# One level of Strassen's recursion in a gate-and-up projection, with the weight differences on GpSimd

## The chip, the cores and the metric

The kernel runs on one core of a Trainium2 chip. That core has a matrix engine (TensorE, PE in the profile), VectorE (DVE), ScalarE (ACT), GpSimd (POOL) and SyncE (SP), which here only issues transfers. They share an on-chip memory, SBUF, of 128 partitions; matmul results go to PSUM, eight banks of 128 x 512 f32. Each engine works its own queue of instructions in order, and waits on semaphores for the others. The metric is the device time of one execution in microseconds.

## What is computed

A hybrid layer (a recurrent branch and an attention branch, merged, then a gated feed-forward), and behind it a second attention layer, on 256 tokens of width 2048, all in f32. The part that matters here is the feed-forward of the first layer:

```python
def _layer(h, ...):
    ...
    h = h + merged @ w_o
    gate, up = jnp.split(_rms(h, n2) @ w_gu, 2, axis=-1)
    return h + (jax.nn.silu(gate) * up) @ w_dn
```

`w_gu` is 2048 x 11264, gate and up each 5632 columns; `w_dn` is 5632 x 2048.

## The kernel before

**Three matmuls for one.** f32 operands are split into two parts of type fp32r, `hi` (a rounded copy, made on ScalarE) and `lo` (what is left, a subtraction on VectorE); that is `split`, lines 219 to 221. `mm3` (line 270) then adds hi x hi, hi x lo and lo x hi into one PSUM bank. All products run in this way, so most matmuls of the profile carry line 263, that of the helper `mm`.

**Weights.** `wload` (line 225) loads one chunk, 256 rows by 512 columns or 512 KB, into a raw tile [128, 1024] by a transfer on SyncE's queue, and splits it. From the output projection on there are two rings of three raw tiles, `raw` and `raw2`, drawn alternately, and three pairs of `hi` and `lo`. The loads and splits are issued with a priority offset `AHEAD` of 300, so that the program's scheduler puts them ahead of the matmuls before them.

**A projection.** `gemm_b` (line 286) takes two banks of tag `g`, one for each half of 128 tokens (t = 0, 1). For each chunk it calls `mm3` for two row blocks and both halves: 12 matmuls of 128x512 on one split chunk. Banks: four of tag `g`, two of `q`, two of `f`.

**The feed-forward** (lines 1009 to 1045). The normalised activations, transposed, are `fgh` and `fgl`, [128, 16, 256] each: 16 row blocks by 256 tokens. The loop at line 1018 makes two passes, over 6 and then 5 groups of 512 hidden columns. A group calls `gemm_b` for the gate (8 chunks, line 1025), makes tanh on ScalarE and the silu on VectorE out of PSUM (lines 1028, 1029), calls it for the up part (line 1030) and multiplies from PSUM (line 1032). `nat_to_t` (line 928) transposes the 512 columns on TensorE into two banks taken from `q` and `f` in turn and splits them again. After each pass the down projection adds its part to the residual `hn` (`add_rows`, line 984).

The order of the instructions on each engine is made when the program is built, by a list scheduler with a model of time.

Of the kernel before, what the change touches and what calls it, by code (L numbers as in the profile page):

```python
# [196 lines left out]
def body(tc, a, out):  # L197
# [5 lines left out]
    with ExitStack() as top:  # L203
# [94 lines left out]
            return [p[:, :n] for p in ps]  # L298

        ch = lambda w, g, c0, c1: [w[g, c] for c in range(c0, c1)]  # L300


        vec = T(cp, [128, NVEC], "vec")
# [621 lines left out]
            flip[0] ^= 1  # L925
            return bank("qf"[flip[0]])

        def nat_to_t(src, hi, lo, kt0, gain=None):

            n = src.shape[2] // 128  # L930
            for k in range(0, n, 2):
                m = min(2, n - k)
                ps = bank2()
                for j in range(m):
                    for t in range(2):
                        o = 256 * j + 128 * t
                        tr(ps[:, o:o + 128], src[:, t, 128 * (k + j):128 * (k + j) + 128], ident)
                if gain is None:
                    split(ps[:, :256 * m].rearrange("p (a b) -> p a b", b=256), hi[:, kt0 + k:kt0 + k + m], lo[:, kt0 + k:kt0 + k + m])
                    continue  # L940
                for j in range(m):
                    kt = kt0 + k + j
                    pj = ps[:, 256 * j:256 * j + 256]
                    S.activation(hi[:, kt], pj, AF.Copy, scale=vc(gain, kt))
                    V.scalar_tensor_tensor(out=lo[:, kt], in0=pj, scalar=vc(gain, kt), in1=hi[:, kt].bitcast(F32), op0=ALU.mult, op1=ALU.subtract)
# [5 lines left out]
        with ExitStack() as ph:  # L951
            mp = ph.enter_context(tc.tile_pool(name="mp", bufs=2))
            mh, ml = unit("Y0", yp), unit("Y1", yp)
            br = []
            for k_, w_, n_, p_ in ((0, "w_a", "X3", yp), (1, "w_b", "X1", xp)):
                u_ = T(p_, [128, 2, 8, 256], n_, F32R)
                br.append((a[w_], u_))
            part = T(xp, [128, 2, D], "X0")
            for b in (1, 0):
                w_, u_ = br[b]  # L960
                for k in range(2):
                    raw = T(wp, [128, 1024], "raw", bufs=3)
                    nc.sync.dma_start(raw.rearrange("p (q f) -> p q f", f=512), ydr[b][2 * k:2 * k + 2].rearrange("q p f -> p q f"))
                    r3_ = raw.rearrange("p (k t) -> p k t", t=256)
                    split(r3_, u_[:, 0, 4 * k:4 * k + 4], u_[:, 1, 4 * k:4 * k + 4])
                for n in range(4):
                    g_ = T(wp, [128, 2, 512], "gate", bufs=1)
                    G.dma_start(g_, gdr[4 * b + n])
                    ps = gemm_b(ch(w_, n, 0, 4), lambda kt: (u_[:, 0, kt], u_[:, 1, kt]))
                    sl = slice(512 * n, 512 * n + 512)  # L970
                    if b == 0:
                        with tc.issue_after(latest[0].ins):
                            nc.sync.dma_start(hn[:, :, sl], a["xn"][:, :, sl])
                    for t in range(2):
                        if b:
                            V.tensor_tensor(out=part[:, t, sl], in0=g_[:, t], in1=ps[t], op=ALU.mult)
                        else:
                            V.tensor_tensor(out=g_[:, t], in0=g_[:, t], in1=ps[t], op=ALU.mult)
                            V.tensor_tensor(out=part[:, t, sl], in0=part[:, t, sl], in1=g_[:, t], op=ALU.add)
                    if b == 0:  # L980
                        nat_to_t(part[:, :, sl], mh, ml, 4 * n)
            sq2 = T(cp, [128, 2, 4], "sq2")

            def add_rows(ps, n, stat, p):
                sl = slice(512 * n, 512 * n + 512)
                for t in range(2):
                    V.tensor_tensor(out=hn[:, t, sl], in0=ps[t], in1=hn[:, t, sl], op=ALU.add)
                    if stat is not None:
                        junk = T(p, [128, 512], "junk")
                        S.activation(junk, hn[:, t, sl], AF.Square, accum_out=stat[:, t, n:n + 1])  # L990

            def rstd(stat, tag, n):
                r = T(cp, [128, 2], tag)
                V.tensor_reduce(out=r, in_=stat, axis=AX.X, op=ALU.add)
                S.activation(r, r, AF.Sqrt, bias=e6, scale=1.0 / n)
                V.reciprocal(r, r)
                return r

            gh, gl = unit("X0", xp), unit("X1", xp)
            more_raw.extend((yp, True))  # L1000
            for n in range(4):
                ps = gemm_b(ch(a["w_o"], n, 0, 8), lambda kt: (mh[:, kt], ml[:, kt]))
                add_rows(ps, n, sq2, mp)
                nat_to_t(hn[:, :, 512 * n:512 * n + 512], gh, gl, 4 * n, "n2")
            r2 = rstd(sq2, "r2", D)


        with ExitStack() as ph:
# [6 lines left out]
            units = (("X2", yp), ("X3", yp), ("Y0", yp), ("Y1", yp), ("X2", yp), ("X3", yp))  # L1015
            ui = 0
            fgh, fgl = gh, gl
            for p0, p1 in ((0, 6), (6, 11)):
                hid = []
                for n in range(p0, p1):  # L1020
                    if (n - p0) % 2 == 0:
                        hid.append(T(units[ui][1], [128, 2, 8, 256], units[ui][0], F32R))
                        ui += 1
                    xg = lambda kt: (fgh[:, kt], fgl[:, kt])
                    pgt = gemm_b(ch(a["w_gu"], n, 0, 8), xg)
                    th = T(fp, [128, 2, 512], "th")
                    for t in range(2):
                        S.activation(th[:, t], pgt[t], AF.Tanh, scale=r2h[:, t:t + 1])  # L1028
                        V.scalar_tensor_tensor(out=th[:, t], in0=th[:, t], scalar=1.0, in1=pgt[t], op0=ALU.add, op1=ALU.mult)
                    pup = gemm_b(ch(a["w_gu"], 11 + n, 0, 8), xg)  # L1030
                    for t in range(2):
                        V.scalar_tensor_tensor(out=th[:, t], in0=pup[t], scalar=r2s[:, t:t + 1], in1=th[:, t], op0=ALU.mult, op1=ALU.mult)
                    hu = hid[-1]
                    nat_to_t(th, hu[:, 0], hu[:, 1], 4 * ((n - p0) % 2))
                last = p1 == 11
                if last:
                    gh, gl = unit("X0", xp), unit("X1", xp)
                for n in range(4):
                    ps = gemm_b(ch(a["w_dn"], n, 2 * p0, 2 * p1), lambda kt: (hid[kt // 8][:, 0, kt % 8], hid[kt // 8][:, 1, kt % 8]))
                    add_rows(ps, n, sq3 if last else None, fp)  # L1040
                    if last:
                        nat_to_t(hn[:, :, 512 * n:512 * n + 512], gh, gl, 4 * n, "np")
# [267 lines left out]
```

## Time and profile before

| what | us |
|---|---|
| median of three runs (2030.91 to 2040.93) | 2037.02 |
| the profiled execution | 2035.52 |
| its span in the profile | 2033.8 |
| one gate-and-up group, from one to the next in the chain | 44.4 |

A row of the profile gives the line, the engine, the operation, the tiles written and read with their shapes, and the count; behind the first bar the busy time in us, the mean of one in ns; behind the second the idle time of that engine just before it and what ended it. In rows of the timeline the first two numbers are start and length in us; neighbours of one kind are merged, with their count. A matmul's duration there overlaps the next one's. In a row of the waits, the total, the count and the longest follow the names.

### The profile page before, as it was taken

The page shows a single profiled execution, that of the slowest core. Times are in us where ns is not written, and L with a number is a line of the kernel's source. Part 1 is how long each engine was busy: PE and PEld are TensorE (multiplying, and loading weights), DVE is VectorE, ACT ScalarE, POOL GpSimd, SP SyncE. Part 2 cuts the span into 40 slices and gives each one's busy share as a digit, 9 for nine tenths or more (in the row PEclk, how much of TensorE's full clock was granted, in tenths as well). Part 3 has the DMA queues.
Part 4 walks back from the last instruction along what each step waited for, and adds up shares of the span by engine and source line. Part 5 has one row for each costly group of instructions (what it writes and reads, how often), then busy time and mean ns, then how long its engine had stood idle before and what let it go on. Part 6 is the DMA issues. An engine that isn't in the chain of part 4 may idle for free.

```text
span 2033.8 us, 29647 instructions
## 1 busy us (share of the span) xinstructions
PE 1981.4 (97%) x11410; PEld 1698.3 (84%) x11410; DVE 1223.3 (60%) x2188; ACT 954.3 (47%) x1290; POOL 152.6 (8%) x226
## 2 busy tenths in 40 slices
PE   8998989999999999999999999999999999999998
PEld 7997879879767778888888888888888889998886
DVE  6787767778755456555555544555555655656555
ACT  6545445546444434554444433444444565444443
POOL 3131041221310000000000000000000000000000
PEclk9999999999999999999999999999999999999999
DMA  6644354444456676555555555555555565444564
GB/s 210 188 131 135 113 162 139 149 152 156 127 157 224 219 265 239 187 187 192 190 186 188 194 189 194 196 187 186 190 193 186 178 205 190 146 135 156 186 193 143
DMA packets 119566, 363.27 MB, mean 179 GB/s; under 512 B 28848, under 2 KB 29648, under 8 KB 119424
## 3 DMA queue, kind: packets, MB, share of 16 engines
q1 hardware_dynamic: 114576, 345.40, 51.7%
q0 software_dynamic: 4848, 15.97, 2.7%
q8 instruction: 89, 1.46, 0.3%
q14 instruction: 53, 0.43, 0.1%
HBM read 351.72 MB, written 9.60 MB: 178 GB/s over the span
## 4 chain that ended last, share of the span: by engine, by line
PE 86%; DVE 6%; DMA 4%; ACT 2%; issue 1%; POOL 1%; SPq 0%; DVEq 0%; ACTq 0%
PE g L263 78%; PE f L263 3%; DVE lo L221 3%; PE q L263 3%; DMA raw<-in_w_b 1%; PE f L267 1%; ACT hi L220 1%; PE q L267 1%; DVE xx L658 1%; DMA raw<-in_w_a 1%; POOL p L854 1%; DVE c L655 1%; DMA raw<-in_w_g 0%; DMA x<-in_xT 0%; DVE gt L589 0%
## 5 line engine op out<-in xcount | busy, mean ns | idle before, releaser
L221 DVE TENSOR_TENSOR lo<-raw,hi 128x1024 fp32r<-128x1024 f32 (+1 forms) x635 | 772.9, 1218 | 604.4 <-ACT hi L220 599.9
L263 PE MATMUL g<-hi,X 128*128 128x512 f32 (+1 forms) x3344 | 1045.5, 391 | 4.3 <-ACT X L220 1.7
L220 ACT CAST hi<-raw 128x1024 fp32r<-128x1024 f32 (+1 forms) x635 | 661.4, 1042 | 817.5 <-PE g L263 679.9
L263 PEld LDWEIGHTS g<-hi,X 128*128 128x128 f32 x3344 | 626.7, 188 | 135.0 <-issue 3.1
L263 PE MATMUL g<-lo,X 128*128 128x512 f32 (+1 forms) x1672 | 652.9, 391 | 2.7 <-DVE lo L221 2.7
L263 PE MATMUL g<-X,hi 128*128 128x272 f32 (+3 forms) x2176 | 430.3, 296 | 3.3 <-ACT hi L220 3.1
L263 PEld LDWEIGHTS g<-lo,X 128*128 128x128 f32 x1672 | 314.3, 188 | 67.5 <-DVE lo L221 5.1
L263 PEld LDWEIGHTS g<-X,hi 128*128 128x128 f32 (+1 forms) x2176 | 347.1, 193 | 10.7 <-ACT hi L220 3.6
L263 PE MATMUL g<-X,lo 128*128 128x272 f32 (+3 forms) x1088 | 318.2, 292 | 1.5 <-DVE lo L221 1.4
L263 PEld LDWEIGHTS g<-X,lo 128*128 128x128 f32 (+1 forms) x1088 | 209.4, 192 | 2.8 <-DVE lo L221 2.4
L263 PE MATMUL g<-hi,Y 128*128 128x512 f32 x544 | 171.0, 391 | 0.0
L263 PEld LDWEIGHTS g<-hi,Y 128*128 128x128 f32 x544 | 102.2, 188 | 20.7
L263 PE MATMUL g<-lo,Y 128*128 128x512 f32 x272 | 106.7, 392 | 0.0
L1049 POOL DMA_DIRECT2D cst<-in_cst x1 | 0.5, 541 | 832.6 <-DMA raw<-in_w_cq 832.6
L263 PEld LDWEIGHTS g<-lo,Y 128*128 128x128 f32 x272 | 51.1, 188 | 10.3
L854 POOL TENSOR_SCALAR p<-ckb,cq,qs 128x144 f32<-128x144 f32 (+1 forms) x32 | 45.6, 1434 | 66.2 <-DVE c L655 28.3
L655 DVE TENSOR_TENSOR c<-hq,xx 108x42 f32<-108x42 f32 (+31 forms) x236 | 40.3, 204 | 9.7 <-DMA hq<-hd 9.4
L658 DVE TENSOR_TENSOR xx<-xx,c 108x42 f32<-108x42 f32 (+31 forms) x236 | 40.8, 203 | 0.4
L420 POOL TENSOR_TENSOR d<-z 128x272 f32<-128x272 f32 (+3 forms) x28 | 22.4, 800 | 86.8 <-DVE z L419 56.0
L870 ACT ACTIVATE p<-p,fst,qs 128x144 f32<-128x144 f32 (+1 forms) x32 | 17.7, 553 | 7.8 <-DVE fst L869 7.6
L267 PE MATMUL f<-ident,p 128*128 128x128 f32 (+1 forms) x64 | 14.5, 333 | 6.6 <-DVE p L873 4.0
L1028 ACT ACTIVATE th<-g,r2h 128x512 f32<-128x512 f32 x22 | 15.1, 685 | 9.9 <-PE g L263 9.9
(425 smaller groups left out, 1342.9 us busy)
## 6 DMA issues: line engine op xcount, KB each, us to landing
raw<-in_w_gu SPq DMA_DIRECT2D x176, 512.0 KB
raw<-in_w_A SPq DMA_DIRECT2D x98, 512.0 KB
raw<-in_w_dn SPq DMA_DIRECT2D x88, 512.0 KB
raw<-in_w_g SPq DMA_DIRECT2D x64, 512.0 KB
raw<-in_w_o SPq DMA_DIRECT2D x32, 512.0 KB
raw<-in_w_qk SPq DMA_DIRECT2D x32, 512.0 KB
raw<-in_w_out SPq DMA_DIRECT2D x32, 512.0 KB
raw<-in_w_b SPq DMA_DIRECT2D x16, 512.0 KB
```

The costliest lines, as they stand in the source:

```text
L220: S.copy(hi, src)
L221: V.tensor_tensor(out=lo, in0=src, in1=hi.bitcast(F32), op=ALU.subtract)
L263: P.matmul(o, l, r, start=start, stop=stop, **k)
L267: P.transpose(o, i, eye)
L420: G.tensor_tensor(out=d[:m, t1:], in0=z[:m, t1:L], in1=z[:m, 1 + t1:], op=ALU.subtract)
L655: V.tensor_tensor(out=t_, in0=hs[:108, j, j + 1:].unsqueeze(1).to_broadcast([108, k_, w]), in1=xs[:, :, j:j + 1].to_broadcast([108, k_, w] ...
L658: V.tensor_tensor(out=xs[:, :, j + 1:], in0=xs[:, :, j + 1:], in1=t_, op=ALU.add)
L854: G.tensor_scalar(out=m_, in0=ckb[:, 2 * j + e, :n], scalar1=cq[:, t, hg:hg + 1], scalar2=qs[:, 0, t, 2 * j + e:2 * j + e + 1], op0=ALU.su ...
L870: S.activation(m_, m_, AF.Exp, bias=st[:, 1, sidx:sidx + 1], scale=qs[:, 1, t, h:h + 1], accum_out=st[:, 2, sidx:sidx + 1])
L1028: S.activation(th[:, t], pgt[t], AF.Tanh, scale=r2h[:, t:t + 1])
L1049: G.dma_start(cst2, a["cst2"])
```

## The change

Gate and up columns are now made together by `gemm_s`, which takes the 8 gate chunks `c1` and the 8 up chunks `c2` of a group. The 8 chunks form four pairs (c, c + 4). Pairs 1 and 3 run as before: each chunk split by `wload`, 48 matmuls a pair. Pairs 0 and 2 run by Strassen's scheme in Winograd's form: the two halves of tokens by the two chunks of rows is one 2 x 2 block matrix, the two chunks by gate and up another. Seven products stand in for eight; each product has six matmuls (two row blocks, three matmuls each).

For that, the four raw weight chunks of a pair are combined on GpSimd by four subtractions of 128x1024 f32 (`t1`, `b12` in place, `t2`, `t4`), and each of the seven right operands is split into hi and lo. The left operands need sums of the activations, made once before the first group by `sums_x` on GpSimd (four combinations a pair) and split. The products go to all eight banks; m1, m5, m6 and m7 are combined by one copy on ScalarE and four additions on VectorE after pair 2, and m2, m3, m4 and m8 are added at the end of pair 3. Gate and up then lie in SBUF tiles `e0` and `e1`, and the silu reads them there. The transposes of a group use a single bank of tag `f`; `junk`, `th`, `e0` and `e1` have one buffer each.

```diff
+        def raw_w(src):
+            more_raw[1] = not more_raw[1]
+            raw = T(wp, [128, 1024], "raw", bufs=3) if more_raw[1] else T(more_raw[0], [128, 1024], "raw2", bufs=3)
+            latest[0] = nc.sync.dma_start(raw.rearrange("p (n m) -> p n m", m=512), src)
+            return raw
+
+        def halves_w(raw):
+            hi, lo = (T(wp, [128, 1024], k, F32R, bufs=3) for k in ("hi", "lo"))
+            split(raw, hi, lo)
+            return tuple(t.rearrange("p (n m) -> p n m", m=512) for t in (hi, lo))
+
+        def sums_x(hi, lo, c, h, p, dst):
+            af = T(p, [128, 2, 2, 256], "T", bufs=3)
+            for k in range(2):
+                ks = slice(2 * (c + k * h), 2 * (c + k * h) + 2)
+                G.tensor_tensor(out=af[:, k], in0=hi[:, ks].bitcast(F32), in1=lo[:, ks].bitcast(F32), op=ALU.add)
+            blk = lambda t, k: af[:, k, :, 128 * t:128 * t + 128]
+            sf = T(p, [128, 4, 2, 128], "T", bufs=3)
+            G.tensor_tensor(out=sf[:, 0], in0=blk(1, 0), in1=blk(1, 1), op=ALU.add)
+            G.tensor_tensor(out=sf[:, 1], in0=sf[:, 0], in1=blk(0, 0), op=ALU.subtract)
+            G.tensor_tensor(out=sf[:, 2], in0=blk(0, 0), in1=blk(1, 0), op=ALU.subtract)
+            G.tensor_tensor(out=sf[:, 3], in0=blk(0, 1), in1=sf[:, 1], op=ALU.subtract)
+            split(sf, dst[0], dst[1])
+
+        def gemm_s(c1, c2, hi, lo, sx, p, e0, e1):
+            h = len(c1) // 2
+            m1, m6, m7, m5 = (bank("g") for _ in range(4))
+            m2, m3, m4, m8 = bank("q"), bank("q"), bank("f"), bank("f")
...
+            for c in range(h):
+                end = c == h - 1
+                if c in sx:
+                    with tc.high_priority(offset=AHEAD):
+                        b12, b11, b22, b21 = (raw_w(v) for v in (c2[c], c1[c], c2[c + h], c1[c + h]))
+                        t1, t2, t4 = (T(p, [128, 1024], "T", bufs=3) for _ in range(3))
+                        G.tensor_tensor(out=t1, in0=b12, in1=b11, op=ALU.subtract)
+                        G.tensor_tensor(out=b12, in0=b22, in1=b12, op=ALU.subtract)
+                        G.tensor_tensor(out=t2, in0=b22, in1=t1, op=ALU.subtract)
+                        G.tensor_tensor(out=t4, in0=b21, in1=t2, op=ALU.subtract)
+                    s_ = [[v[:, k] for v in sx[c]] for k in range(4)]
+                    stop = c == last
+                    for ps, l, r, st in (
+                        (m1, blk(0, c), b11, stop), (m2, blk(0, c + h), b21, False), (m3, s_[3], b22, False),
+                        (m5, s_[0], t1, stop), (m7, s_[2], b12, stop), (m6, s_[1], t2, stop), (m4, blk(1, c + h), t4, False),
+                    ):
+                        with tc.high_priority(offset=AHEAD):
+                            r = halves_w(r)
+                        prod(ps, l, r, st)
+                    if stop:
+                        S.copy(e0[:, 0], m1)
+                        V.tensor_tensor(out=e0[:, 1], in0=m6, in1=e0[:, 0], op=ALU.add)
+                        V.tensor_tensor(out=e1[:, 0], in0=m5, in1=e0[:, 1], op=ALU.add)
+                        V.tensor_tensor(out=e0[:, 1], in0=m7, in1=e0[:, 1], op=ALU.add)
+                        V.tensor_tensor(out=e1[:, 1], in0=m5, in1=e0[:, 1], op=ALU.add)
+                    continue
+                for src, k, ps in ((c1[c], c, (m2, m4)), (c1[c + h], c + h, (m2, m4)), (c2[c], c, (m3, m8)), (c2[c + h], c + h, (m3, m8))):
+                    r = wload(src, 2, 512)
+                    for t in range(2):
+                        prod(ps[t], blk(t, k), r, end and k >= h)
+                    if end and k >= h:
+                        e_ = e0 if ps[0] is m2 else e1
+                        for t in range(2):
+                            V.tensor_tensor(out=e_[:, t], in0=ps[t], in1=e_[:, t], op=ALU.add)
...
-                    xg = lambda kt: (fgh[:, kt], fgl[:, kt])
-                    pgt = gemm_b(ch(a["w_gu"], n, 0, 8), xg)
-                    th = T(fp, [128, 2, 512], "th")
+                    e0, e1 = T(fp, [128, 2, 512], "e0", bufs=1), T(wp, [128, 2, 512], "gate", bufs=1)
+                    gemm_s(ch(a["w_gu"], n, 0, 8), ch(a["w_gu"], 11 + n, 0, 8), fgh, fgl, sx, fp, e0, e1)
+                    th = T(fp, [128, 2, 512], "th", bufs=1)
                     for t in range(2):
-                        S.activation(th[:, t], pgt[t], AF.Tanh, scale=r2h[:, t:t + 1])
-                        V.scalar_tensor_tensor(out=th[:, t], in0=th[:, t], scalar=1.0, in1=pgt[t], op0=ALU.add, op1=ALU.mult)
-                    pup = gemm_b(ch(a["w_gu"], 11 + n, 0, 8), xg)
-                    for t in range(2):
-                        V.scalar_tensor_tensor(out=th[:, t], in0=pup[t], scalar=r2s[:, t:t + 1], in1=th[:, t], op0=ALU.mult, op1=ALU.mult)
+                        S.activation(th[:, t], e0[:, t], AF.Tanh, scale=r2h[:, t:t + 1])
+                        V.scalar_tensor_tensor(out=th[:, t], in0=th[:, t], scalar=1.0, in1=e0[:, t], op0=ALU.add, op1=ALU.mult)
+                        V.scalar_tensor_tensor(out=th[:, t], in0=e1[:, t], scalar=r2s[:, t:t + 1], in1=th[:, t], op0=ALU.mult, op1=ALU.mult)
                     hu = hid[-1]
-                    nat_to_t(th, hu[:, 0], hu[:, 1], 4 * ((n - p0) % 2))
+                    nat_to_t(th, hu[:, 0], hu[:, 1], 4 * ((n - p0) % 2), ps=bank("f"))
```

More of the change, by code (lines that the diff above doesn't have):

```diff
@@ new lines, in gemm_s, with prod @@
+        def gemm_s(c1, c2, hi, lo, sx, p, e0, e1):
+            h = len(c1) // 2
+            m1, m6, m7, m5 = (bank("g") for _ in range(4))
+            m2, m3, m4, m8 = bank("q"), bank("q"), bank("f"), bank("f")
+            used = set()
+            def prod(ps, l, r, stop=False):
+                for j in range(2):
+                    mm3(ps, [v[:, j] for v in l], [v[:, j] for v in r], id(ps) not in used, stop and j == 1)
+                    used.add(id(ps))
+            blk = lambda t, c: [v[:, 2 * c:2 * c + 2, 128 * t:128 * t + 128] for v in (hi, lo)]
+            last = max(c for c in range(h) if c in sx)
+            for c in range(h):
[32 more added lines that the diff above has]
+                            V.tensor_tensor(out=e_[:, t], in0=ps[t], in1=e_[:, t], op=ALU.add)
@@ L926, in bank2, with nat_to_t @@
             return bank("qf"[flip[0]])
-        def nat_to_t(src, hi, lo, kt0, gain=None):
-            n = src.shape[2] // 128
+        def nat_to_t(src, hi, lo, kt0, gain=None, ps=None):
+            n, one = src.shape[2] // 128, ps
             for k in range(0, n, 2):
                 m = min(2, n - k)
-                ps = bank2()
+                ps = bank2() if one is None else one
                 for j in range(m):
@@ L988, in add_rows @@
                     if stat is not None:
-                        junk = T(p, [128, 512], "junk")
+                        junk = T(p, [128, 512], "junk", bufs=1)
                         S.activation(junk, hn[:, t, sl], AF.Square, accum_out=stat[:, t, n:n + 1])
@@ L1017, in body @@
             fgh, fgl = gh, gl
+            sx = {}
+            for c in (0, 2):
+                sx[c] = tuple(T(fp, [128, 4, 2, 128], f"S{c}", F32R, bufs=2) for _ in range(2))
+                sums_x(fgh, fgl, c, 4, fp, sx[c])
             for p0, p1 in ((0, 6), (6, 11)):
```

## The prediction

> **What bounds the kernel now.** I read the page's first part, then the chain that ended last, then the busy time by stretches of one gate-and-up group each, then the waits.
>
> ```profile
> span 2033.8 us, 29647 instructions
> PE 1981.4 (97%) x11410; PEld 1698.3 (84%) x11410; DVE 1223.3 (60%) x2188; ACT 954.3 (47%) x1290; POOL 152.6 (8%) x226
> ```
> ```profile
> 931.04 43.31 PE g L263 x191
> 975.46 43.33 PE g L263 x191
> ```
> ```profile
> core 0: us, PE busy (x) PEld busy (x) DVE busy (x) ACT busy (x) POOL busy (x), PEclk, DMA share, GB/s
> 975.40:1019.90 44.50, 44.50 (x202) 36.93 (x201) 23.49 (x22) 19.13 (x21) 0.00 (x0) 1.00 0.58 190
> ```
> TensorE bounds the stage. The chain runs on it without a break: 191 matmuls in 43.31 us, which is 0.2268 us from one matmul to the next (the 391 ns that the page gives for one overlap with its neighbours and must not be used as a price). One group of 512 gate and 512 up columns recurs every 975.46 - 931.04 = 44.42 us: 192 x 0.2268 = 43.5, and 0.9 for eight transposes. In that time VectorE is busy 23.5 us, ScalarE 19.1, GpSimd not at all, and the DMA engines 58%.
>
> ```profile
> ACT hi L220 <- PE g L263: 679.9, 433, 7.8
> DVE lo L221 <- ACT hi L220: 599.9, 476, 5.6
> ```
> ```profile
> L221 DVE TENSOR_TENSOR lo<-raw,hi 128x1024 fp32r<-128x1024 f32 x618 | 759.0, 1229 | 592.3 <-ACT hi L220 587.8 <-PE f L267 1.7
> L220 ACT CAST hi<-raw 128x1024 fp32r<-128x1024 f32 x618 | 649.7, 1051 | 808.1 <-PE g L263 676.0 <-issue 41.9 <-DMA raw<-in_w_b 23.2
> L1032 DVE SCALAR_TENSOR_TENSOR th<-g,r2s,th 128x512 f32<-128x512 f32 x22 | 15.4, 744 | 0.0
> L987 DVE TENSOR_TENSOR Y<-g,Y 128x512 f32<-128x512 f32 x24 | 15.4, 682 | 0.0
> L1029 DVE SCALAR_TENSOR_TENSOR th<-th,g 128x512 f32<-128x512 f32 x22 | 15.1, 684 | 5.3 <-ACT th L1028 5.3
> ```
> Every weight chunk is split into hi (ScalarE, 1.05 us) and then lo (VectorE, 1.23 us). ScalarE waits for TensorE to free one of three hi/lo pairs, and VectorE waits for ScalarE. So the two splitters have slack now: one split of 2.28 us for 12 matmuls, 2.72 us.
>
> **What the change does to TensorE.** Two of four chunk pairs go from 48 matmuls to 7 x 6 = 42. Per group 12 fewer, in 11 groups 132, by 0.2268: 29.9 us less. A group is then 180 x 0.2268 + 0.9 = 41.7 us of TensorE. That is all there is to gain, and only while TensorE stays the bound.
>
> **What it adds on VectorE and ScalarE.** Per group 22 splits stand in place of 16, and eight evictions that combine the products (PSUM and one tile of SBUF, 0.68 us each by the L987 row), with the four L1029/L1032 operations and two transposed lo's of 0.69 staying. VectorE: 22 x 1.23 = 27.1, + 8 x 0.68 = 5.5, + 2.9, + 1.4 = 36.8 us of 41.7. ScalarE: 22 x 1.05 + about 3.2 = 26.3. By their own sums both still fit. The seven products of a pair take 6 x 0.2268 = 1.36 us each, and each needs a lo of 1.23: there VectorE is all but full, so anything that holds it up shows on TensorE.
>
> **What it adds on GpSimd.** Four two-input operations of 128x1024 f32 per pair, eight per group, 88 in all. The trace has no such size; the nearest rows, of GpSimd (POOL) and of VectorE in the same stretches:
>
> ```profile
> 10.32 1.35 POOL L350 TENSOR_TENSOR x<-x 128x544 f32<-128x544 f32 x1 [5.49 <-ACT x L349]
> ...
> 318.60 0.61 POOL L420 TENSOR_TENSOR d<-z 128x256 f32<-128x256 f32 x1
> ```
> ```profile
> L855 POOL TENSOR_TENSOR p<-p,cst x32: 447/459/1548, 145.3 to 553.9; 128x128 f32<-128x128 f32 x32
> ```
> ```profile
> 215.90 1.22 DVE L221 TENSOR_TENSOR lo<-raw,hi 128x1024 fp32r<-128x1024 f32 x1
> 217.03 1.28 DVE L552 TENSOR_TENSOR x<-t 128x32 f32<-128x32 f32 x1
> ...
> 216.15 2.11 POOL L564 TENSOR_TENSOR t<-t 128x512 f32<-128x512 f32 x1 [2.43 <-DVE x L550]
> ```
> ```profile
> 368.73 0.18 DVE L552 TENSOR_TENSOR x<-t 128x32 f32<-128x32 f32 x1
> ```
> ```profile
> 24.36 1.31 DVE L221 TENSOR_TENSOR lo<-raw,hi 128x672 fp32r<-128x672 f32 x1 [0.63 <-ACT hi L220]
> 28.41 0.86 DVE L221 TENSOR_TENSOR lo<-raw,hi 128x672 fp32r<-128x672 f32 x1 [2.74 <-ACT hi L220]
> ```
> ```profile
> 22.11 2.84 POOL L350 TENSOR_TENSOR x<-x 128x544 f32<-128x544 f32 x1 [2.69 <-ACT x L349]
> ```
> These rows carry the forecast. At 215.90 VectorE runs a lo until 217.12. GpSimd's L564 starts at 216.15 and ends at 218.26, 1.14 us behind the lo's end. VectorE's next operation, the tiny L552, which takes 0.18 us elsewhere, starts at 217.03 and ends at 218.31, together with GpSimd's. So a lo and a GpSimd operation with two SBUF inputs **do not overlap: they take turns**. The same at 24.36: a 672-wide lo takes 1.31 in place of 0.86, ending behind the L350 that ran until 24.95; and that L350 took 2.84 in place of 1.35, because lo's ran first.
>
> The skill states this as a rule: the Trainium skill, "SBUF — State Buffer", section "Who interferes with whom", says that a VectorE instruction with two SBUF inputs contends with a GpSimd instruction that reads SBUF, that whichever is first holds the shared pair for its whole length, and that one SBUF input does not contend. By its last clause the evictions run beside GpSimd; without that clause, with evictions and transposed lo's taking turns too, the group's sum below would be 6.9 us more (the serial sum among the rivals).
>
> ```profile
> 311.71 1.50 POOL L420 TENSOR_TENSOR d<-z 128x272 f32<-128x272 f32 x1
> ...
> 312.64 0.60 DVE L732 TENSOR_TENSOR g__3686<-q,x 64x128 f32<-64x128 f32 x2
> 593.41 0.61 DVE L732 TENSOR_TENSOR g__6959<-q,x 64x128 f32<-64x128 f32 x2 [0.65 <-PE q L263]
> ```
> The row at 312.64 agrees with that clause: VectorE operations with one input in PSUM take the same 0.60 beside L420's turn as with GpSimd idle (593.41).
>
> How long is a turn of 128x1024? From the 512-wide operation behind the lo, 2 x 1.14 = **2.28 us**. Below: from 128 to 256 elements costs 0.15, so 0.61 + 6 x 0.15 = 1.5. Above: from 256 to 544, 2.57 ns an element, so 1.35 + 480 x 2.57 ns = 2.6. I take 2.28, as 512 is the nearest width that was seen in a turn.
>
> **The sum.** Turns per group: 22 lo's 27.1, the four L1029/L1032 operations (both inputs are in SBUF after the change; L1029 and L1032 read PSUM before) 2.9, eight differences 8 x 2.28 = 18.2. Together **48.2 us**, more than TensorE's 41.7 and than the 44.4 of now. The shared turn becomes the bound.
>
> On top comes time in which nobody takes the turn. The ring holds six raw tiles. In a pair, the fifth product's split frees the tile that the third plain chunk needs, and the next pair's loads queue behind that one on SyncE. Counted from a pair's start, that split ends at about 8.3 (five lo's of 1.23 and two differences left from before, less the lo's that were made ahead); four loads of 512 KB at 190/0.58 = 328 GB/s take 1.6 each, 6.4 together; with 1.3 for issue, the next pair's first difference can start near 16. The lo's of the pair and of the first two plain chunks are done near 13.4, one more fills 1.2: some 1.2 us free per pair, **2.4 per group**. Its bounds: 0 (loads land early), and 6 (they land 3.2 us later: 512 KB issued from GpSimd landed after 4.8 us, against the 1.6).
>
> ```profile
> gdr<-gate POOLq DMA_DIRECT2D x8, 512.0 KB, 4.8
> ```
> A group becomes 48.2 + 2.4 = 50.6, which is 6.2 more than 44.4; by 11 groups 68 us. At the start of the stage GpSimd makes sums of the activations (4 operations of 512 and 8 of 256, about 4 x 1.25 + 8 x 0.61 = 10 us); half lie under the last output projection, and two of the first differences need scratch tiles that the second half frees: 4 us, between 0 and 10. The transposes of a group now use one PSUM bank for both halves, so the second half may wait for a split (0.59 + 0.69, about 1.8 with the hand-overs): between 0 and 20 us over 11 groups; I take 0, since TensorE is no longer the bound and has matmuls of the next pair to do meanwhile; without that cover it is 20. The bank waits of the products cost 0: evictions have at least two products, 2.7 us, before the bank is needed again, and without that cover 0.7 each time. Weight traffic, the down projection and everything outside lines 1018 to 1034 stay.
>
> Sum: 2035.5 (the profiled execution, span 2033.8) + 68 + 4 = **2107 us**. The median of the three runs, 2037.0, is 1.5 above that execution; I leave the sum as it is.
>
> **Rivals.**
> TensorE stays the bound (the other side). 2035.5 - 29.9 + 4 = 2010, with 2 for late splits 2012. It needs a turn under (41.7 - 30.0)/8 = 1.5 us with no free time at all, the lower bound of the rows, or GpSimd's reads hidden beside lo's, which the rows at 24.36 and 216.15 speak against. For it speaks that each turn of a plain chunk has slack: 2.72 us for one lo.
> A short turn. At 1.5 us a turn the group is 30.0 + 12 + 2.4 = 44.4, as now: 2040, within what can be told.
> The differences come late. If nothing overlaps, VectorE's 36.8 and GpSimd's 18.2 add to 55.0 a group: 2035.5 + 11 x 10.6 + 4 = 2156. If, worse, all four differences of a pair fall between its seven lo's, a pair takes 8.6 + 9.1 = 17.7 and its plain half 10.9, 59 a group with the tail: 2200. For it: the differences cannot start before about 16 of 25 us. Against: a plain half needs only four lo's in 10.9 us.
> The clock falls as TensorE waits.
>
> ```profile
> 100.00:200.00 100.00, 91.98 (x821) 83.72 (x819) 78.20 (x263) 47.12 (x83) 26.55 (x35) 0.95 0.42 129
> ```
> With TensorE busy 92% of that stretch the granted clock was 0.95, against 1.00 in the gate-and-up stage. At 41.7 of 50.6, 82%, a clock of 0.95 costs 2.2 us a group if none of it is hidden: 2131. The Trainium skill, "TensorE: Matmul & The Clock Gate", Part 1, says that the clock is halved after an idle window of about 3.4 us; by that rule single waits of 1 to 2 us, which is what I expect, leave it whole.
>
> **How the numbers follow.** The forecast, 2107 (own range 2075 to 2140, by free time 0 to 6 and the turn 2.28 to 2.6): 0.62. Late differences, 2156 to 2200: 0.18. The clock, 2131: 0.06. TensorE still the bound, 2012: 0.09. The short turn, 2040: 0.05. The range 2060 to 2170 leaves out the last two and the end of the late case, under 0.2 together. A measurement of this kernel can tell about 0.5%, 10 us, from no change. Faster 0.09, the same 0.05, slower 0.86.
>
> **What would show it.** In the profile after, in the gate-and-up stage: TensorE's matmuls fall by 132, yet its busy share falls to near 82%, and it waits for lo. The mean of lo rises above 1.23 (it waits for the turn inside its own duration), GpSimd is busy eight times a group with means well above 2.3. Groups recur every 50 us or so. It would be wrong if lo stays at 1.23 beside a busy GpSimd (no turns), if GpSimd's operation takes under 1.5 us, or if the stage is shorter than 44.4 a group; the waits would then name TensorE again.

## The result, and the profile after

The changed kernel takes **2096.5 us** (median of four runs, 2095.9 to 2104.6) beside 2036.8 before: a ratio of 1.0305, with a 95% interval of 1.0269 to 1.0341. The forecast was 2107, in a range of 2060 to 2170. The profiled execution took 2096.8 us, 61.3 more than the 2035.5 of before; the spans differ by 61.2.

The page of the changed kernel, span and busy time by engine, and the chain that ended last:

```profile
span 2095.0 us, 29913 instructions
...
PE 1982.8 (95%) x11278; PEld 1668.2 (80%) x11278; DVE 1501.7 (72%) x2344; ACT 1029.2 (49%) x1369; POOL 432.1 (21%) x326
...
PE 64%; DVE 18%; issue 10%; ACT 3%; DMA 3%; POOL 1%; SPq 1%; DVEq 0%; ACTq 0%; POOLq 0%
```

There are 132 matmuls fewer, as announced, and yet the span is longer. TensorE's "busy" total did not fall either (1981.4 before): the records model where a matmul ends, and one behind a gap is drawn longer (0.50 us behind the wait of 2.87 before 1143.65, 0.39 where matmuls follow each other). The count and the chain say more. TensorE's share of the chain was 86% before and is 64% now; VectorE's rose from 6% to 18%, and 10% is "issue", where the chain finds no releaser. In the group from 1062 to 1112 that is 40.8%, nearly all of it while a lo is under way: no semaphore shows what such a lo waits for.

Where do the 61.2 us lie? The tanh of each group is a good milestone. The timeline of ScalarE, first of the kernel before, then of the changed one: start, length, instruction; the first and the last of its eleven groups.

```profile
903.09 0.69 ACT L1028 ACTIVATE th<-g,r2h 128x512 f32<-128x512 f32 x1
...
1477.63 0.69 ACT L1028 ACTIVATE th<-g,r2h 128x512 f32<-128x512 f32 x1 [0.98 <-PE g L263]
```
```profile
941.72 1.34 ACT L1111 ACTIVATE th<-e,r2h 128x512 f32<-128x512 f32 x2 [3.12 <-DVE e L379]
...
1557.18 1.33 ACT L1111 ACTIVATE th<-e,r2h 128x512 f32<-128x512 f32 x2
```

From the first group to the last it was 574.5 us and is 615.5, so **ten intervals cost 40.9**, 4.1 each. The first tanh comes 38.6 later, and from the last tanh to the end there are 18.3 fewer (556.2 and 537.8), since tanh now stands behind the up part as well. The two together are 20.3: the first group's own 4.1, and **16.2 us up to the start of the stage and in it**. 40.9 + 20.3 = 61.2. The last matmul of the output projection, before and after, tells these two apart:

```profile
880.35 0.39 PE L263 MATMUL g<-hi,Y 128*128 128x512 f32 x1
```
```profile
876.51 0.39 PE L263 MATMUL g<-hi,Y 128*128 128x512 f32 x1
```

The changed kernel reached the stage 3.8 us earlier, so the start itself cost 20.0. Whether the change had a part in the 3.8 is open: there is one profile of each kernel, and the times of one kernel differ by up to 10 us.

A steady group, by the windows view of the changed kernel (one group, from near one tanh to the next):

```profile
core 0: us, PE busy (x) PEld busy (x) DVE busy (x) ACT busy (x) POOL busy (x), PEclk, DMA share, GB/s
1062.10:1111.40 49.30, 44.56 (x189) 33.82 (x189) 48.31 (x37) 25.61 (x27) 23.16 (x9) 1.00 0.52 171
```

VectorE is busy 48.3 of 49.3 us, where the prediction counted 36.8 of its own work, and the granted clock is whole. Why VectorE is that busy, the groups by line and form show:

```profile
L221 DVE TENSOR_TENSOR lo<-raw,hi 128x1024 fp32r<-128x1024 f32 x618 | 897.9, 1460 | 376.9 <-ACT hi L220 372.0 <-PE f L267 1.8
...
L354 POOL TENSOR_TENSOR T<-raw,T 128x1024 f32<-128x1024 f32 x22 | 74.3, 3379 | 0.0
...
L352 POOL TENSOR_TENSOR T<-raw,raw 128x1024 f32<-128x1024 f32 x22 | 61.3, 2784 | 360.2 <-DMA raw<-in_w_gu 330.0 <-DVE e L367 30.3
```

The mean of lo rose from 1229 to 1460 ns, over all its uses in the kernel. In the stage alone (941.72 to 1183.81) it is 195.0 us for 110 of them, 1.77 each, where the kernel before has 106.9 for 88, 1.21. The four differences take 2.7 to 3.4 us. One stretch of the timeline of the changed kernel, VectorE and, in the second block, GpSimd, shows both at once:

```profile
1078.52 3.19 DVE L221 TENSOR_TENSOR lo<-raw,hi 128x1024 fp32r<-128x1024 f32 x1
1081.64 0.68 DVE L368 TENSOR_TENSOR gate<-g,e 128x512 f32<-128x512 f32 x1
1082.24 2.92 DVE L221 TENSOR_TENSOR lo<-raw,hi 128x1024 fp32r<-128x1024 f32 x1
...
1085.68 2.81 DVE L221 TENSOR_TENSOR lo<-raw,hi 128x1024 fp32r<-128x1024 f32 x1
...
1097.76 1.21 DVE L221 TENSOR_TENSOR lo<-T,hi 128x1024 fp32r<-128x1024 f32 x1
1098.90 1.21 DVE L221 TENSOR_TENSOR lo<-raw,hi 128x1024 fp32r<-128x1024 f32 x1
1100.03 1.21 DVE L221 TENSOR_TENSOR lo<-T,hi 128x1024 fp32r<-128x1024 f32 x1
```
```profile
1078.22 2.41 POOL L352 TENSOR_TENSOR T<-raw,raw 128x1024 f32<-128x1024 f32 x1 [10.60 <-DMA raw<-in_w_gu]
1081.67 2.40 POOL L353 TENSOR_TENSOR raw<-raw,raw 128x1024 f32<-128x1024 f32 x1 [1.04 <-DMA raw<-in_w_gu]
1084.03 3.38 POOL L354 TENSOR_TENSOR T<-raw,T 128x1024 f32<-128x1024 f32 x1
1087.49 3.27 POOL L355 TENSOR_TENSOR T<-raw,T 128x1024 f32<-128x1024 f32 x1
```

Read the two side by side. The difference at 1078.22 has the turn until 1080.63; the lo begun at 1078.52 ends 1.08 behind it, at 1081.71, after 3.19 us. The next difference runs 1081.67 to 1084.07, and the lo of 1082.24 ends at 1085.16, 1.09 behind it. The third difference starts at 1084.03, gets nothing before that lo is through, and shows 3.38. A record thus holds the wait for the turn and the work; 2.40 us is a difference that begins with the turn free. The eviction L368, with one input in PSUM, takes its 0.68 beside the difference at 1081.67.

The waits of the changed kernel (total us, count, longest):

```profile
DVE lo L221 <- ACT hi L220: 392.4, 347, 5.1
...
PEld q L263 <- DVE lo L221: 58.2, 54, 3.3
PE q L263 <- DVE lo L221: 36.2, 47, 2.9
...
PE g L263 <- DVE lo L221: 16.8, 29, 2.5
```

VectorE's wait for hi fell from 599.9 to 392.4 us, and TensorE's matmuls now wait for lo, 53 us in the two rows of PE. The row of PEld is largely the same idle time once more, as the weight load beside such a matmul waits with it.

The start of the stage, on TensorE, on GpSimd, and by the windows view, all of the changed kernel:

```profile
888.41 0.79 PE L263 MATMUL q<-hi,S 128*128 128x512 f32 x1 [7.88 <-ACT S L220]
...
894.68 0.79 PE L263 MATMUL g<-hi,S 128*128 128x512 f32 x1 [2.71 <-ACT hi L220]
...
897.98 0.80 PE L263 MATMUL g<-lo,S 128*128 128x512 f32 x1 [2.50 <-DVE lo L221]
```
```profile
879.51 2.49 POOL L322 TENSOR_TENSOR T<-X,X 128x512 f32<-128x512 f32 x2 [102.03 <-ACT junk L1069]
...
890.51 0.73 POOL L328 TENSOR_TENSOR T<-T 128x256 f32<-128x256 f32 x1
891.20 2.36 POOL L352 TENSOR_TENSOR T<-raw,raw 128x1024 f32<-128x1024 f32 x1
```
```profile
880.00:915.00 35.00, 20.33 (x70) 14.29 (x69) 26.70 (x18) 14.00 (x17) 30.07 (x19) 0.76 0.32 104
```

GpSimd makes the sums of both pairs in one piece, from 879.51 to 891.2, and the first difference only behind them. TensorE has two products (12 matmuls) that need no sum, waits 7.88 us for the first, and then twice some 2.6. In this stretch the granted clock is 0.76.

### The profile page after: what moved, and what is told of

The parts are those of the page before. It is cut to its first block, busy times and chain, and to the rows that moved or that the text cites. A ratio compares the mean times of both kernels' runs of the same rounds, so it can differ in the third digit from the quotient of the medians.

```text
span 2095.0 us, 29913 instructions
## 1 busy us (share of the span) xinstructions
PE 1982.8 (95%) x11278; PEld 1668.2 (80%) x11278; DVE 1501.7 (72%) x2344; ACT 1029.2 (49%) x1369; POOL 432.1 (21%) x326
## 4 chain that ended last, share of the span: by engine, by line
PE 64%; DVE 18%; issue 10%; ACT 3%; DMA 3%; POOL 1%; SPq 1%; DVEq 0%; ACTq 0%; POOLq 0%
PE g L263 54%; DVE lo L221 10%; PE q L263 5%; PE f L263 3%; ACT hi L220 2%; PE f L267 1%; DVE th L1112 1%; DVE c L734 1%; DVE xx L737 1%; PE q L267 1%; POOL p L933 1%; DVE X L221 0%; DVE gt L668 0%; DMA x<-in_xT 0%; DMA hq<-hd 0%
## 5 line engine op out<-in xcount | busy, mean ns | idle before, releaser
L221 DVE TENSOR_TENSOR lo<-raw,hi 128x1024 fp32r<-128x1024 f32 (+1 forms) x635 | 911.8, 1443 | 389.6 <-ACT hi L220 384.6
L263 PE MATMUL g<-hi,X 128*128 128x512 f32 (+1 forms) x2024 | 640.2, 391 | 3.2 <-ACT X L220 1.7
L263 PEld LDWEIGHTS g<-hi,X 128*128 128x128 f32 x2024 | 378.3, 188 | 82.7 <-issue 2.6
L263 PE MATMUL g<-lo,X 128*128 128x512 f32 (+1 forms) x1012 | 396.6, 392 | 10.6 <-DVE lo L221 10.5
L263 PEld LDWEIGHTS g<-X,hi 128*128 128x128 f32 (+1 forms) x2176 | 345.6, 192 | 10.7 <-ACT hi L220 4.0
L263 PEld LDWEIGHTS g<-lo,X 128*128 128x128 f32 x1012 | 190.1, 188 | 57.5 <-DVE lo L221 20.8
L263 PE MATMUL q<-hi,X 128*128 128x512 f32 x440 | 155.8, 395 | 0.0
L263 PE MATMUL f<-hi,X 128*128 128x512 f32 x440 | 150.1, 390 | 0.0
L352 POOL TENSOR_TENSOR T<-raw,raw 128x1024 f32<-128x1024 f32 x22 | 61.3, 2784 | 360.2 <-DMA raw<-in_w_gu 330.0
L263 PE MATMUL q<-lo,X 128*128 128x512 f32 x220 | 91.0, 414 | 30.8 <-DVE lo L221 30.7
L263 PE MATMUL g<-hi,S 128*128 128x512 f32 x264 | 90.6, 405 | 2.7 <-ACT hi L220 2.7
L221 DVE TENSOR_TENSOR lo<-T,hi 128x1024 fp32r<-128x1024 f32 x66 | 83.5, 1279 | 7.9 <-ACT hi L220 7.8
```

What stands on the lines that cost most here:

```text
L221: V.tensor_tensor(out=lo, in0=src, in1=hi.bitcast(F32), op=ALU.subtract)
L263: P.matmul(o, l, r, start=start, stop=stop, **k)
L352: G.tensor_tensor(out=t1, in0=b12, in1=b11, op=ALU.subtract)
```

## The experiments

The changed kernel is the base of all; each diff is against it. Ratios are to the kernel before, whose medians beside them were 2034.8 to 2035.8. The theory: operations of GpSimd that read SBUF and VectorE's operations with two SBUF inputs take turns, and the sum of the turns is the group. The first rivals: VectorE is full by its own work, and the differences merely come too late.

**Without the differences.**

```diff
-                        t1, t2, t4 = (T(p, [128, 1024], "T", bufs=3) for _ in range(3))
-                        G.tensor_tensor(out=t1, in0=b12, in1=b11, op=ALU.subtract)
...
+                        t1, t2, t4 = b11, b22, b21
```

> The four differences of each pair are left out: products m5, m6 and m4 take the raw chunks themselves, so the output is not the reference's. Theory 'turns' (GpSimd's two-input operations and VectorE's two-input operations exclude each other): the mean of lo goes back to 1.23 us, a gate-and-up group lasts 42 to 43.5 us (TensorE's own sum is 41.7, VectorE's 36.8) and the time is 2036.8 + 10 (start) + 11 x (42.5 - 44.4), about 2026, between 2015 and 2037. Theory 'VectorE is full by its own work' (22 splits, eight evictions and a ring of three hi/lo pairs): the group stays at 47 to 49 us, time 2075 to 2096. Theory 'late differences' agrees with 'turns' here.

2022.5 us, ratio 0.9932 (0.9906 to 0.9957). The group of lo, a window from one tanh to the next, and TensorE's one wait at the start:

```profile
L221 DVE TENSOR_TENSOR lo<-raw,hi 128x1024 fp32r<-128x1024 f32 x684 | 836.4, 1228 | 461.3 <-ACT hi L220 451.4 <-PE f L267 1.7 <-PE q L263 1.2
```
```profile
977.90:1019.70 41.80, 41.80 (x190) 34.50 (x189) 34.60 (x36) 25.75 (x29) 0.00 (x0) 1.00 0.58 204
```
```profile
898.38 0.79 PE L263 MATMUL q<-hi,S 128*128 128x512 f32 x1 [10.02 <-ACT S L220]
```

All splits, products and evictions are still there, and a group takes 41.8, TensorE's own sum of 41.7. VectorE is busy 34.6 of it: it is not full by its own work. Ten intervals are 26.1 us shorter than before; the start is still late, by 17.7 against a group that is 2.6 shorter. Of this, 4.0 lie ahead of the stage (the last matmul of the output projection starts at 884.34), and 13.7 in it, with the sums alone: TensorE waits 10.02 us for them. With free differences, but with this start, the change is worth 0.7%.

**GpSimd busy with writes only:** nine memsets a pair in place of the four differences.

```diff
-                        G.tensor_tensor(out=t1, in0=b12, in1=b11, op=ALU.subtract)
...
+                        for _ in range(3):
+                            G.memset(t1, 0.5)
```

> In place of the four differences GpSimd fills t1, t2 and t4 three times each with a constant (nine memsets of 128x1024 a pair, about 1.0 us each, so about as busy as with the differences); b12 goes into its product as loaded, so the output is not the reference's. GpSimd is busy but reads no SBUF. 'Turns', if only reading takes the turn: lo at 1.23, group 42 to 43.5, about 2026. If any busy GpSimd holds VectorE up: lo at 1.4 and more, group 47 to 50, 2075 to 2100.

2027.6, ratio 0.9950 (0.9931 to 0.9968). The groups of lo and of one of the memsets:

```profile
L221 DVE TENSOR_TENSOR lo<-raw,hi 128x1024 fp32r<-128x1024 f32 x618 | 756.4, 1226 | 454.0 <-ACT hi L220 448.0 <-PE f L267 1.7
...
L357 POOL MEMSET T<- 128x1024 f32 x66 | 63.3, 959 | 1.3
```

Three of the four products with a difference now take tiles that GpSimd has written, and lo stays at 1.226, though most of the memsets run beside a lo (33 of 40 us from 1000 to 1100). A busy GpSimd by itself costs nothing in a group, which takes 41.8 us here too. The memsets wait for no load, so this run says nothing on differences that come late.

**One-input copies** in place of the differences, four of 128x1024 a pair.

```diff
-                        G.tensor_tensor(out=t1, in0=b12, in1=b11, op=ALU.subtract)
...
+                        G.tensor_copy(t1, b11)
+                        G.tensor_copy(t2, t1)
+                        G.tensor_copy(t4, t2)
+                        G.tensor_copy(t4, b21)
```

> In place of each of the four two-input differences of a pair GpSimd copies a tile of 128x1024 f32 in SBUF (one input), into t1, t2 and t4, so the output is not the reference's. If every GpSimd instruction that reads SBUF takes VectorE's turn: lo at 1.35 us and more, group 45 to 49, 2050 to 2096. If only GpSimd's two-input operations do: lo at 1.23, group 42 to 43.5, 2020 to 2030. A GpSimd copy may take 1 to 2.4 us; the trace of before has none.

2038.0 in a single run, between the two expectations. A group takes 42.9 us, as by the second. But lo in the stage (941.72 to 1183.81) takes 162.9 us for 120, 1.36 each, as by the first, against 147.5 for 122, 1.21, in the run without differences. The rows over the whole kernel:

```profile
L221 DVE TENSOR_TENSOR lo<-raw,hi 128x1024 fp32r<-128x1024 f32 x618 | 793.9, 1286 | 429.3 <-ACT hi L220 424.1 <-PE f L267 1.7 <-PE q L263 1.2
...
L352 POOL COPY T<-raw 128x1024 f32<-128x1024 f32 x22 | 49.3, 2242 | 296.6 <-DMA raw<-in_w_gu 203.4 <-DVE lo L221 93.2
...
L355 POOL COPY T<-raw 128x1024 f32<-128x1024 f32 x22 | 27.5, 1248 | 108.2 <-DMA raw<-in_w_gu 108.1
```

A copy takes 1.04 us at its fastest and 1.25 in the mean where it mostly has the turn to itself (L355), and 2.24 where it runs among lo's (L352): a GpSimd operation with a single SBUF input takes turns too, with a shorter turn. The rule that the prediction took from the Trainium skill ("SBUF — State Buffer", section "Who interferes with whom") speaks of a GpSimd instruction that reads SBUF, whatever its number of inputs, and excepts one that only writes it. The copies (lo at 1.36 in the stage) and the memsets (1.226) agree with it on both sides.

**The differences on VectorE.**

```diff
-                        G.tensor_tensor(out=t1, in0=b12, in1=b11, op=ALU.subtract)
+                        V.tensor_tensor(out=t1, in0=b12, in1=b11, op=ALU.subtract)
...
```

> The four differences of each pair run on VectorE in place of GpSimd. 'Turns': VectorE's sum is 36.8 + 8 x 1.23 = 46.6 us a group, lo is back at 1.23, the group lasts 46.6 to 48, time about 2079 (2069 to 2088): faster than the changed kernel although VectorE has more to do. 'Late differences' (only GpSimd's 2.4 us per operation and the late loads matter): the differences are ready early, group 42 to 44, time below 2045. 'VectorE full by its own work': 49.3 + 9.8 = 59 a group, about 2200.

2082.9, ratio 1.0224 (1.0152 to 1.0297), inside the expected range. That is the median of two runs, 2078.7 and 2087.2, both below the four of the changed kernel, though the intervals of the two ratios overlap. One engine doing both is no slower than two that take turns, as a difference costs 1.23 there instead of a turn of 2.4. But the number was hit in part by luck. VectorE's own sum of 46.6 does not bound: it is busy 43.1 of 48.0 us from 1000 to 1048. The groups take 47.3 to 47.8, and the rows of L352 and L353 show VectorE standing 11.4 and 10.7 us in all before loads that have not landed. That came back below.

**More turns, first try:** two more GpSimd additions of 128x512 a pair, on the sums of the activations.

```diff
+                        for k in range(2):
+                            idle = T(p, [128, 512], "junk", bufs=1)
+                            xf = [sx[c][k][:, 2 * j:2 * j + 2].bitcast(F32).rearrange("p a b t -> p (a b t)") for j in range(2)]
+                            G.tensor_tensor(out=idle, in0=xf[0], in1=xf[1], op=ALU.add)
```

> The changed kernel with two further GpSimd additions of 128x512 a pair, which read the activation sums and write a tile that nobody reads; they stand behind the four differences, in front of idle time of GpSimd. 'Turns': 2 x 2 x 1.14 = 4.6 us more of the shared turn a group, of which about 1 falls into free time: group 52 to 54, time about 2140 (2125 to 2147). 'Late differences': nothing waits for them and GpSimd idles some 10 us a pair, so group 49.3 and 2096 as before.

2139.0, ratio 1.0500 (1.0440 to 1.0559): inside the range by turns, but not for the reason given. The additions read only constants, so nothing held them, and all ran early. The windows of two groups:

```profile
951.30:1015.60 64.30, 50.78 (x190) 37.12 (x189) 64.30 (x37) 25.68 (x28) 60.82 (x26) 0.89 0.41 131
1080.40:1127.60 47.20, 43.79 (x189) 33.95 (x188) 46.19 (x38) 25.61 (x28) 21.88 (x8) 1.00 0.54 179
```

Two early groups, with up to 26 GpSimd instructions, take 64 us; later ones have about eight again and take 47 to 52. In the early ones the differences queue behind the additions, so they also come late, and this run doesn't part the two theories.

**More turns, behind the differences:** the same number, reading `t4` and `t2`, so that each runs once per pair and behind its differences.

```diff
+                        for k in range(2):
+                            idle = T(p, [128, 512], "junk", bufs=1)
+                            G.tensor_tensor(out=idle, in0=t4[:, 512 * k:512 * k + 512], in1=t2[:, 512 * k:512 * k + 512], op=ALU.add)
```

> As the run with further GpSimd additions, but these read t2 and t4, so they can only run behind a pair's four differences and in front of GpSimd's idle time; they delay no operand. Two of 128x512 a pair, 2 x 2 x 1.14 = 4.6 us more of the shared turn a group. 'Turns': about 2 us of the turn are free in a group of 48.6 us, so a group becomes 51 to 53, time 2124 to 2147. 'Late differences' (what costs is that a product waits for GpSimd): nothing waits for these, 2096 to 2102.

2146.1, ratio 1.0532 (1.0514 to 1.0551). The additions' group and a window from one tanh to the next:

```profile
L358 POOL TENSOR_TENSOR junk<-T 128x512 f32<-128x512 f32 x44 | 88.1, 2002 | 3.4
```
```profile
1451.88:1504.92 53.04, 44.82 (x190) 33.83 (x189) 52.57 (x37) 25.71 (x27) 31.55 (x13) 1.00 0.48 158
```

No product needs these additions and they stand behind what the products need, yet a group takes 53 us. From first to last tanh the time rises from 615.5 to 658.8 (949.78 to 1608.59), so 4.3 for four additions, 1.08 each. Half a turn of 128x1024, by the prediction's row, is 1.14. Some of the 4.3 may be indirect: the additions keep scratch tiles a little longer, L353 waited longer for its loads (37.1 us in all against 18.6), and the granted clock was 0.94 to 0.97 in seven of the ten intervals. In the window shown it was whole. That the differences alone come late is ruled out as the main cause: by it this run would have been 2096 to 2102.

**One pair instead of two**, on GpSimd.

```diff
-            for c in (0, 2):
+            for c in (2,):
```

> Strassen's scheme on pair 2 alone; pair 0 runs as before the change. Differences stay on GpSimd. 'Turns': a group has 19 lo's, four differences: 23.4 + 2.9 + 9.1 = 35.4 us of turns against 43.5 + 0.9 - 6 x 0.2268 = 43.1 of TensorE, so TensorE bounds most of the group; inside the one pair lo's still wait. Group 43.5 to 44.5, start 3 to 6, time about 2036 (2026 to 2045).

2048.7, ratio 1.0063 (1.0043 to 1.0082), 13 more than expected. The start costs only 2.8 us in the stage, but a group takes 45.7 where TensorE's sum is 186 x 0.2268 + 0.9 = 43.1. The turns of the group, 19 lo's and four differences, fit well into 43.1; they don't fit into the one pair where they are bunched: the chain of the group from 1012 to 1058 lies on lo's, and on their waits, from 1033.7 to 1039.0. A sum over the group was the wrong size of box for this version.

**One pair on VectorE**, and the same with the sums of the activations on VectorE too.

```diff
-                        G.tensor_tensor(out=t1, in0=b12, in1=b11, op=ALU.subtract)
+                        V.tensor_tensor(out=t1, in0=b12, in1=b11, op=ALU.subtract)
...
-            for c in (0, 2):
+            for c in (2,):
```

> As the run with one pair, with the four differences on VectorE. VectorE: 33.1 + 4 x 1.23 = 38.0 us a group, under TensorE's 43.1, and no turns in the groups: 43.1 to 43.8 a group, time about 2030 (2022 to 2038). If the one-pair kernel on GpSimd is as fast, turns don't matter below TensorE's sum.

> As the run with one pair and its differences on VectorE, with the sums of the activations made on VectorE too, so GpSimd is out of the stage. The start falls from about 5 us to about 3: 2028 (2020 to 2036).

2082.1 and 2081.8, ratios 1.0227 (1.0207 to 1.0247) and 1.0226 (1.0209 to 1.0242): both some 50 us above what was expected, and as slow as two pairs on VectorE. The groups of the first of them name the cause:

```profile
L352 DVE TENSOR_TENSOR T<-raw,raw 128x1024 f32<-128x1024 f32 x11 | 13.6, 1238 | 16.4 <-DMA raw<-in_w_gu 16.4
...
L355 DVE TENSOR_TENSOR T<-raw,T 128x1024 f32<-128x1024 f32 x11 | 13.5, 1225 | 27.9 <-DMA raw<-in_w_gu 27.9
```

VectorE works its queue in order. The differences stand early in it, before lo's that are ready, and wait there for loads: 16.4 + 13.5 (L353) + 27.9 = 58 us over eleven groups. On GpSimd such a wait held nobody; the wait of L352 there is 330 us.

**The same, queued behind the last lo before the pair**, for one pair and for both.

```diff
+                before_ = last_lo[0]
...
-                        G.tensor_tensor(out=t1, in0=b12, in1=b11, op=ALU.subtract)
+                        with tc.issue_after(before_.ins):
+                            V.tensor_tensor(out=t1, in0=b12, in1=b11, op=ALU.subtract)
...
```

> One pair a group, its four differences on VectorE, and each of them set in VectorE's queue behind the last lo of the chunks before the pair, so that its loads have landed. If the 2082 of the one-pair kernel with differences on VectorE came from VectorE standing before a load that had not landed, with the next lo's queued behind it: VectorE 38.0 a group under TensorE's 43.1, group 43.1 to 43.8, start 2.5, time 2035.5 + 2.5 - 11 x 1.0 = 2027 (2022 to 2036). If VectorE's differences cost more than their 1.23 in some other way: 2060 and more.

> Both pairs of the changed kernel, differences on VectorE, behind the last lo before the pair. VectorE's sum of 46.6 a group bounds: group 46.6 to 47.6, start 17 as in the changed kernel, time 2035.5 + 17 + 11 x 2.6 = 2081 (2070 to 2090). If it comes below 2055, VectorE's sum was not the bound in the run with all differences on VectorE.

One pair: 2044.3, ratio 1.0042 (1.0025 to 1.0058). The groups:

```profile
L355 DVE TENSOR_TENSOR raw<-raw,raw 128x1024 f32<-128x1024 f32 x11 | 13.4, 1220 | 0.1
L354 DVE TENSOR_TENSOR T<-raw,raw 128x1024 f32<-128x1024 f32 x11 | 13.4, 1218 | 0.0
```

The waits for loads are gone and with them 38 us, so the place in the queue was the cause. It is still 17 above the expectation: a group takes 45.7 instead of 43.1 to 43.8, because four differences and the lo's now stand back to back in the pair and TensorE waits for them there (the chain lies on VectorE from 1035.7 to 1044.8).

With both pairs behind (2112.1, ratio 1.0382, 1.0360 to 1.0404) it is 31 above, and a group takes 51.5:

```profile
ACT hi L220 <- DVE T L354: 19.9, 10, 2.4
```

Here the place in the queue does more than was meant. In program order the last split before pair 0 is that of the transposed silu of the group before, so the differences of pair 0 stand behind that (it starts at 1100.20, the first difference at 1100.81). ScalarE waits for that difference once a group, ten times 2 us, TensorE then waits 3.66 us for hi, and the granted clock is 0.90 to 0.93 in the groups. How the loss divides among these no run took apart.

**The first pair of the first group plain**, so that the stage starts with chunks that need no sums.

```diff
-                    gemm_s(ch(a["w_gu"], n, 0, 8), ch(a["w_gu"], 11 + n, 0, 8), fgh, fgl, sx, fp, e0, e1)
+                    gemm_s(ch(a["w_gu"], n, 0, 8), ch(a["w_gu"], 11 + n, 0, 8), fgh, fgl, {2: sx[2]} if n == 0 else sx, fp, e0, e1)
```

> The changed kernel, except that pair 0 of the first group runs without Strassen's scheme, so TensorE does not wait for the sums of the activations at the start. If the start costs 17 us in the changed kernel (TensorE waits 8 us for the sums and runs on with a halved clock), it falls to 2 or 3: time about 2082 (2078 to 2088). If the 17 us belong to something else at the start: 2092 and more.

2090.1, ratio 1.0274 (1.0254 to 1.0294): 6.5 us gained of the 14.5 expected, outside the range and short of the other case too. The longest wait of TensorE at the start is 2.98 us instead of 7.88, and the granted clock from 880 to 915 is 0.95 instead of 0.76. Much of the shortfall lies ahead of the stage: the last matmul of the output projection starts at 882.19 here, 5.7 later than in the changed kernel. Counted from there the start falls from 20.0 us to 8.2. Of these, 1.4 are the six matmuls more; that the others come from sums and first differences that still take turns with the first lo's is argued, not shown.

No version that computes the whole is faster than the kernel before; the nearest is one pair with the differences queued behind, 0.4% slower.

## Why the prediction came out as it did

**TensorE's gain: right.** 132 matmuls fewer, and 41.7 us a group: the run without differences shows 41.8 and a chain that lies on TensorE.

**The shared turn becomes the bound: right, and shown.** It goes away with the differences (lo back at 1.228), stays away when GpSimd only writes (1.226), and grows with more turns (+4.3 us a group).

**The size of a group: 50.6 forecast, less measured.** The ten intervals cost 4.1 us each where the forecast had 6.2, 45 instead of 68 over eleven groups. The steady groups, taken without the interval that spans the first down projection, average 48.6 (five from 941.72 to 1183.81, four from 1361.69 to 1557.18). Three terms make it up. The lo was priced by its duration, 1.23, but lo's that follow each other start every 1.14 (1097.76, 1098.90, 1100.03 above): 25.1 for 22 instead of 27.1. The four operations of silu come to some 2.5 instead of 2.9. The turn of a difference, 2.28 by the 512-wide row, is 2.40 where it stands alone, and in the alternation some 2.35 (3.46 from the difference at 1084.03 to the next, with a lo of 1.1 in it): 18.8 for eight instead of 18.2. Together 46.4. The rows bear this out: from 1062.10 to 1111.40 a lo, a silu operation out of SBUF or a GpSimd operation is under way for 46.1 of the 49.3 us. The 2 to 3 us left match the 2.4 of free time by luck. The prediction meant a VectorE without work behind late loads, but VectorE is idle for 1.0 us of that window; in the rest it evicts from PSUM while GpSimd waits for loads, a term that the prediction had at nothing. The over-estimate is mostly one slip: a **spacing was used for the matmuls and a duration for the lo's**, in the same sum.

**The start: 4 forecast (0 to 10), 16.2 measured, or 20.0 counted from the end of the output projection.** This step failed, outside its own bounds. It priced GpSimd's sums at 10 us, which is near (11.7), and took half of them to lie under the last output projection. None did: the first sum starts at 879.51, after the first gate matmul at 876.74. Its row names `junk` of L1069, the last square sum of the output projection, as what released it. That is no input of the sums; perhaps their scratch tile lies in memory that `junk` still held, but no run tried another place, and in two other runs the profile names another releaser. The step also had nothing for the clock. The run with no differences still loses 13.7 us in the stage, so the sums are most of the cause; with a plain first pair 8.2 are left of the 20.0.

**The two errors half cancel:** 23 too much in the groups and 12 too little at the start make 2107 for 2096.8. That the sum is this near is in part luck.

**TensorE stays the bound:** not so; its terms, with free differences, come out as 2022.5 rather than 2012, by the start again.

**Late differences:** against this rival stand the run with additions behind the differences (+4.3 us a group, where it has nothing) and the rows in which a lo ends 1.08 or 1.09 us behind a difference. Late differences appear where the queue was changed (two early groups of the first run with more turns).

**The clock:** in steady groups it stayed nearly whole: 1.00 in seven, 0.97 and 0.96 in two, where TensorE's longest wait was 2.88 and 2.89 us. At the start it fell to 0.76, behind a wait of 7.88 us, and 0.85 behind the 10.02 of the run without differences. The Trainium skill, "TensorE: Matmul & The Clock Gate", Part 1, which the prediction weighed, halves the clock after an idle window of about 3.4 us. The runs agree in the order of size, but show no sharp limit there: waits of 2.87 us left 1.00 in two other groups of the changed kernel, and a longest wait of 2.5 to 3.5 us a group went with 0.93 to 0.97 in the run with one pair on VectorE, against 1.00 where the longest was 0.70 (queued behind the lo). The prediction applied the rule to the steady state only, and the start is where it bit.

**What was to be seen:** GpSimd eight times a group well above 2.3, and TensorE waiting for lo, came; a busy share of 82% did not show, as the records draw waiting matmuls longer (44.56 of 49.3, 90%).

## What to carry to other kernels

Before elementwise work goes to an idle GpSimd, look at what VectorE does beside it: where its operations have two SBUF inputs, add both engines' SBUF work into one sum, and do so for the shortest stretch in which the work is bunched, not for the whole group. Price steady work by the spacing of starts, on every engine and not on TensorE alone. In an in-order queue an operation that waits for a load holds all that stands behind it, so moving work to the cheaper engine can cost more than the operations; and one-time preparation belongs where its first user is far away.

## What the runs showed of the hardware

A GpSimd subtraction of two 128x1024 f32 tiles takes 2.40 us with the turn free, on VectorE 1.22. A GpSimd copy of that size takes 1.04 with the turn free, yet takes turns with lo's as well (up to 3.12). A memset of that size takes 0.96 and disturbs no lo. With the differences on VectorE, where they are serial by construction, the kernel took 2082.9 us instead of 2096.5 (two runs beside four).
